# Layer 1's attention: TensorE's instructions in a written order, scores two pairs ahead, and a modulation block moved behind the first scores

## The chip, the cores and the metric

The kernel runs on one NeuronCore of a Trainium2 chip. The metric is the device time of one execution in microseconds (us), lower is better. The matrix engine is TensorE (PE in the profile, PEld its weight loads), VectorE is DVE, ScalarE is ACT, GpSimd is POOL, and SyncE (SP) issues the large weight loads. A name with a q (SPq, PEq) is an engine's instruction queue.

## The reference

The program computes two blocks in fp32 over 256 tokens of width 1024. The first block has two layers; the second has a recurrent mixer, a sparse attention and a mixture of experts. The change touches only the attention of layer 1 of the first block: 16 query heads in four groups, 256 tokens in two blocks of 128 queries, each with a window of local keys, 256 context keys and one sink logit per head.

```python
s_loc = jnp.einsum('bkgnqd,bkncd->bkgnqc', qb, kb).astype(f32) * scale
s_loc = jnp.where(valid, s_loc, -jnp.inf)
s_ctx = jnp.einsum('bkgnqd,bkld->bkgnql', qb, k_c).astype(f32) * scale
m = jnp.maximum(jnp.maximum(jnp.max(s_loc, -1, keepdims=True), jnp.max(s_ctx, -1, keepdims=True)), s_sink)
e_loc = jnp.exp(s_loc - m)
e_ctx = jnp.exp(s_ctx - m)
denom = jnp.sum(e_loc, -1, keepdims=True) + jnp.sum(e_ctx, -1, keepdims=True) + jnp.exp(s_sink - m)
o = (jnp.einsum('bkgnqc,bkncd->bkgnqd', e_loc, vb) + jnp.einsum('bkgnql,bkld->bkgnqd', e_ctx, v_c)) / denom
y = merge_heads(window_attention(q, k, v, k_c, v_c, od_sink[j])) @ od_w_out[j]
```

Beside it stands the modulation of the layers: `silu(c) @ w_mod + b_mod`, a vector times large weight matrices, which the kernel computes in blocks of 512 columns spread over the program.

## The kernel before

A tile framework turns the program into five instruction streams: it tracks the data dependencies, adds the semaphores and, for each engine, picks the order by priority (program order, unless a priority is raised) as operands and buffers come free in its plan. So the order on an engine is not the order of the lines; parts of one step can be cut up and mixed with others. Only at the end of the program (the experts) TensorE and SyncE are put in written order with `manual_schedule`.

The attention of layer 1 works on 16 pairs `(cb, tq, m)`: two query heads at a time, 128 queries, 512 keys. For a pair i there are:

- `a_scores` (L1143, L1146): for each of the two heads three matmuls of 64 rows by 512 columns (head 0 on rows 0 to 63 of the array, head 1 on rows 64 to 127; three because operands are split in a high and a low part) into a tile `s` of two PSUM banks, then two bf16 matmuls that add the window mask. There are two `s` tiles.
- `a_max` (L1152 to L1154), on VectorE: the row maximum of both heads, its minimum with the negated sink, and the difference that the sink's exponential needs.
- `a_exp` (L1161 to L1166): on ScalarE two exponentials of 512 columns that also sum up, and one of two columns for the sink; on VectorE the sum (L1163), the reciprocal (L1164) and two scalings of 512 columns (L1166).
- `a_turn` (L1172): eight transposes on TensorE into `pt`, of which there is one tile of two banks.
- `a_evac`: two copies of `pt` to SBUF on ScalarE.
- `a_av` (L1186): eight value matmuls (16 instructions), at a raised priority; after the fourth pair of a group ScalarE and VectorE write the result `o` as a high and a low part (L1190, L1191).

ScalarE's instructions appear under L244 and splits under L251, since helpers record them. The loop is written with scores one pair ahead. At i = 11 GpSimd fetches five row tiles and combines them (`x_of`, L886 and L887). At i = 16, behind the last pair, `fill(1)` puts in one modulation block (`mods_ev`, L398): 32 matmuls (64 instructions) over two 1 MB tiles that SyncE loaded (`wload`, L259, a ring of five `wr` buffers), a bias row, and an addition on VectorE (L400).

After the attention come the output projection (`mm_t`, L344 to L346), two more modulation blocks and the feed-forward part of layer 1.

Of the kernel before, what the change touches and what calls it, by code (L numbers as in the profile page):

```python
# [13 lines left out]
AF = mybir.ActivationFunctionType  # L14
# [102 lines left out]
def emit(tc, I, out, taps=None, stop=None):  # L117
# [64 lines left out]
    def t4(dt=F32, shape=(128, 1024)):  # L182
        return ap_.tile(list(shape), dt, name=nm("t4_"), tag="b4", bufs=NB["b4"])
# [59 lines left out]
    def act(o, i, fn, **k):  # L243
        return ac.activation(o, i, fn, **k)  # L244
# [622 lines left out]
    def brow1024(src_ap, eng=None):  # L867
        t_ = t4()
        (eng or po).dma_start(t_, bass.AP(tensor=src_ap.tensor, offset=src_ap.offset, ap=[[0, 128], [1, 1024]]))
        return t_  # L870
# [13 lines left out]
    def x_of(z, rows):  # L884

        po.tensor_tensor(z, z, rows[0], op=OP.mult)  # L886
        po.tensor_tensor(z, z, rows[1], op=OP.add)  # L887

    def tok_rows(d, t):
        return d[t * 128:(t + 1) * 128, :]  # L890
# [3 lines left out]
        ve.tensor_mul(tmp, ps, gate[:, cs])  # L894
        ve.scalar_tensor_tensor(z[:, cs], z[:, cs], ALPHA, tmp, op0=OP.mult, op1=OP.add)

    NF = (0, 2.2, 1, 2, 2, (16,))

    fills = [(1, 0), (1, 2), (1, 1), (1, 3), (1, 4), (1, 5), (1, 6), (1, 8), (1, 7), (1, 9), (2, 0), (2, 2), (2, 1), (2, 3),
             (2, 4), (1, 10), (1, 11), (2, 5), (2, 6), (2, 8), (2, 7), (2, 9), (2, 10), (2, 11)]  # L900
# [234 lines left out]
    def a_scores(i):  # L1135
        cb, tq, m = pairs[i]
        s_ = T_[i]["s"] = pst("s", (128, 2, 512))
        qs = slice(m * 256 + tq * 128, m * 256 + tq * 128 + 128)
        ks = slice(cb * 512, cb * 512 + 512)
        for hd in range(2):  # L1140
            pr = slice(64 * hd, 64 * hd + 64)
            for j, (qp, kp) in enumerate(((0, kTh), (0, kTl), (1, kTh))):
                pe.matmul(s_[:, hd], qT[cb][qp][pr, qs], kp[pr, ks], start=j == 0, stop=False, skip_group_check=True)  # L1143
        wc = slice(128, 256) if tq == 0 else slice(0, 128)
        for hd in range(2):
            pe.matmul(s_[:, hd, wc], identb, wmb[:, tq], start=False, stop=True, skip_group_check=True)  # L1146

    def a_max(i):
        cb, tq, m = pairs[i]
        nmx = T_[i]["nmx"] = sm((128, 4))  # L1150
        nsk = nsink[:, cb * 8 + 2 * m:cb * 8 + 2 * m + 2]
        ve.tensor_reduce(nmx[:, 0:2], T_[i]["s"], axis=AX.X, op=OP.max, negate=True)  # L1152
        ve.tensor_tensor(nmx[:, 0:2], nmx[:, 0:2], nsk, op=OP.min)
        ve.tensor_sub(nmx[:, 2:4], nmx[:, 0:2], nsk)  # L1154

    def a_exp(i):
        s_, nmx = T_[i]["s"], T_[i]["nmx"]
        e, den = t4(), sm((128, 4))
        T_[i]["e"] = e
        for hd in range(2):  # L1160
            act(e[:, HF[hd]], s_[:, hd], AF.Exp, bias=nmx[:, hd:hd + 1], accum_out=den[:, hd:hd + 1])  # L1161
        act(den[:, 2:4], nmx[:, 2:4], AF.Exp)
        ve.tensor_add(den[:, 0:2], den[:, 0:2], den[:, 2:4])  # L1163
        ve.reciprocal(den[:, 0:2], den[:, 0:2])  # L1164
        for hd in range(2):
            ve.tensor_scalar(e[:, HF[hd]], e[:, HF[hd]], den[:, hd:hd + 1], None, op0=OP.mult)  # L1166

    def a_turn(i):
        pt = T_[i]["pt"] = pst("t", (128, 4, 2, 128))
        for hd in range(2):  # L1170
            for c in range(4):
                pe.transpose(pt[:, c, hd], T_[i]["e"][:, c128(4 * hd + c)], ident)  # L1172

    def a_evac(i):
        pT = T_[i]["pT"] = t4(F32, (128, 4, 2, 128))
        act(pT[:, 0:2], T_[i]["pt"][:, 0:2], AF.Copy)
        act(pT[:, 2:4], T_[i]["pt"][:, 2:4], AF.Copy)

    def a_av(i):
        cb, tq, m = pairs[i]  # L1180
        o = T_[i]["o"] = pst("o", (128, 4, 128)) if m == 0 else T_[i - 1]["o"]
        with tc.high_priority(60):
            for c in range(4):
                for hd in range(2):
                    v0 = c * 256 + (2 * cb + hd) * 64
                    pe.matmul(o[64 * hd:64 * hd + 64, m, :], vT[:, v0:v0 + 64], T_[i]["pT"][:, c, hd], start=c == 0,  # L1186
                              stop=c == 3, skip_group_check=True, tile_position=(0, 64 * hd))
        if m == 3:
            hi, lo = aT.span(cb * 4, 4, tq * 128, tq * 128 + 128)
            act(hi, o, AF.Copy)  # L1190
            ve.tensor_sub(lo, o, hi.bitcast(F32))  # L1191

    N_ = len(pairs)
    a_scores(0)
    a_max(0)
    for i in range(N_ + 1):
        if i + 1 < N_:
            a_scores(i + 1)
        if i < N_:
            a_exp(i)  # L1200
        if i >= 1:
            a_evac(i - 1)
        if i + 1 < N_:
            a_max(i + 1)
        if i >= 1:
            a_av(i - 1)
        if i < N_:
            a_turn(i)
        if i == 11:
            g1 = brow1024(mods_dram[1][0, 2048:3072])  # L1210
            lnr = [brow1024(I["ln_g"][0, 1]), brow1024(I["ln_b"][0, 1])]
            z = [t4() for _ in range(2)]
            for t in range(2):
                po.dma_start(z[t], tok_rows(xres1, t))
                x_of(z[t], lnr)
        if i in NF[5]:
            fill(1, lambda shape: pst("o", shape))
    psum_tags(g=4, x=4)

    tap("aT0", aT.hi[0].bitcast(F32))  # L1220
# [1114 lines left out]
```

## Time and profile before

| | us |
|---|---|
| median of 3 executions | 1558.17 (1555.2 to 1563.67) |
| the profiled execution | 1555.63 |
| its span, first to last instruction | 1553.9 |
| TensorE busy | 1440.3 (93%) |
| VectorE busy | 971.8 (63%) |
| ScalarE busy | 549.2 (35%) |
| GpSimd busy | 263.7 (17%) |

The profile is of one execution; 1.7 us of its time lie outside of the span. [...] A busy TensorE in the records is not one at its peak: ends of matmuls are modelled and overlap, so the distance between starts is what to read. Averages over the span say little on one stage; the attention is read from its own windows.

### The profile page before, as it was taken

To read this page: it belongs to the slowest core of one execution; us is meant where nothing else is said; L and a number is where in the kernel's file an instruction comes from. 1 tells how busy PE (TensorE), PEld (TensorE's weight loads), DVE (VectorE), ACT (ScalarE), POOL (GpSimd) and SP (SyncE) were. 2 spreads that over 40 slices of the span, in tenths; PEclk is the share of its full clock that TensorE was granted. 3 is DMA by queue.
4 is the path that set the end of the run, shared out by engine and by line. 5 is a ranking of instruction groups with operands and counts; after the bars stand their busy time and mean duration, and the time that the engine had idled before them with its cause. 6 is when DMAs were issued, how large, how long until landed. Compare 5 with 4: busy or idle time off the path is not lost. (4 is left out here: it accounts for less than half of the span.)

```text
span 1553.9 us, 22193 instructions
## 1 busy us (share of the span) xinstructions
PE 1440.3 (93%) x8651; PEld 1081.8 (70%) x8651; DVE 971.8 (63%) x1662; ACT 549.2 (35%) x921; POOL 263.7 (17%) x263
## 2 busy tenths in 40 slices
PE   5999899999999999989889899997898897999896
PEld 3688687798887778869657898986787675532332
DVE  2443797789999887685665766566688446112212
ACT  2443233353223223234454455545554333301001
POOL 0032204100132210321130410003425320000000
PEclk9998999999999999999889999998999798999999
DMA  8740564446779876526323965564334746699996
GB/s 290 261 167 1 190 244 143 162 151 216 236 258 326 279 239 224 207 72 191 84 69 107 331 214 190 190 213 154 116 110 138 255 152 240 251 410 410 411 410 259
DMA packets 189395, 332.96 MB, mean 214 GB/s; under 512 B 12666, under 2 KB 67554, under 8 KB 189283
## 3 DMA queue, kind: packets, MB, share of 16 engines
q1 hardware_dynamic: 175152, 298.77, 55.4%
q0 software_dynamic: 8640, 27.85, 5.1%
q10 hardware_dynamic: 5490, 4.85, 1.1%
q8 instruction: 70, 1.15, 0.3%
q14 instruction: 43, 0.34, 0.1%
HBM read 320.91 MB, written 10.53 MB: 213 GB/s over the span
## 5 line engine op out<-in xcount | busy, mean ns | idle before, releaser
L251 DVE TENSOR_TENSOR wl<-wr,wh 128x1024 fp32r<-128x1024 f32 (+1 forms) x206 | 254.1, 1247 | 65.8 <-ACT wh L244 63.9
L244 ACT ACTIVATE wh<-wr 128x1024 fp32r<-128x1024 f32 (+1 forms) x226 | 228.8, 1027 | 176.0 <-PE g L346 91.3
L344 PE MATMUL g<-wh,h 128*128 128x512 f32 (+1 forms) x624 | 247.5, 399 | 13.0 <-DVE t L1396 7.1
L319 PE MATMUL g<-h,wh 128*128 128x256 f32 (+1 forms) x768 | 251.7, 329 | 3.5 <-DVE t L1031 2.4
L321 PE MATMUL g<-h,wl 128*128 128x256 f32 (+1 forms) x768 | 250.2, 327 | 3.8 <-DVE wl L251 3.8
L320 PE MATMUL g<-h,wh 128*128 128x256 f32 (+1 forms) x768 | 251.2, 328 | 0.2 <-DVE h L251 0.2
L345 PE MATMUL g<-wl,h 128*128 128x512 f32 (+1 forms) x624 | 244.9, 393 | 2.6 <-DVE wl L251 2.6
L346 PE MATMUL g<-wh,h 128*128 128x512 f32 (+1 forms) x624 | 244.2, 393 | 2.0 <-DVE h L1701 2.0
L427 DVE SCALAR_TENSOR_TENSOR t<-wr,cT,t 128x512 f32<-128x512 f32 x231 | 172.8, 785 | 14.2 <-DMA wr<-w_mod_in 7.0
L319 PEld LDWEIGHTS g<-h,wh 128*128 128x128 f32 x768 | 147.3, 192 | 20.0 <-DVE t L1031 3.7
L321 PEld LDWEIGHTS g<-h,wl 128*128 128x128 f32 x768 | 147.2, 192 | 17.2 <-DVE wl L251 5.1
L320 PEld LDWEIGHTS g<-h,wh 128*128 128x128 f32 x768 | 147.6, 192 | 12.5 <-DVE h L251 0.6
L344 PEld LDWEIGHTS g<-wh,h 128*128 128x128 f32 x624 | 119.2, 192 | 42.9 <-issue 10.1
L345 PEld LDWEIGHTS g<-wl,h 128*128 128x128 f32 x624 | 119.2, 191 | 26.9 <-DVE wl L251 3.8
L346 PEld LDWEIGHTS g<-wh,h 128*128 128x128 f32 x624 | 118.8, 190 | 27.1 <-DVE h L1701 3.0
L244 ACT ACTIVATE t<-t 128x512 f32<-128x512 f32 (+7 forms) x83 | 47.3, 592 | 129.3 <-DVE t L2163 73.6
L244 ACT ACTIVATE h<-e 128x512 fp32r<-128x512 f32 (+1 forms) x64 | 33.5, 524 | 146.1 <-DVE e L962 146.1
L251 POOL TENSOR_TENSOR wl<-wr,wh 128x1024 fp32r<-128x1024 f32 x20 | 50.4, 2519 | 192.2 <-ACT wh L244 180.4
L244 ACT ACTIVATE t<-x 128x128 f32<-128x128 f32 (+3 forms) x78 | 30.7, 464 | 145.0 <-PE x L2139 109.7
L244 ACT ACTIVATE e<-g 128x512 f32<-128x512 f32 (+1 forms) x72 | 35.6, 494 | 95.2 <-PE g L321 85.6
L241 POOL TENSOR_TENSOR sm<-sm,mhalf 128x1 f32<-128x1 f32 (+2 forms) x33 | 33.1, 1004 | 160.9 <-DVE sm L238 122.7
L2132 PE MATMUL g<-wr,t 128*32 128x512 f32 (+1 forms) x248 | 49.9, 596 | 6.3 <-DMA wr<-w_in 6.1
(429 smaller groups left out, 2180.1 us busy)
## 6 DMA issues: line engine op xcount, KB each, us to landing
wr<-mlp_w_in SPq DMA_DIRECT2D x64, 1024.0 KB
wr<-w_mod_in SPq DMA_DIRECT2D x40, 1024.0 KB
wr<-w_in SPq DMA_DIRECT2D x32, 1024.0 KB
t<-w_in SPq DMA_DIRECT2D x52, 512.0 KB
wr<-w_ada_in SPq DMA_DIRECT2D x24, 1024.0 KB
wr<-w_in_in SPq DMA_DIRECT2D x16, 1024.0 KB
wx<-w_in SPq DMA_DIRECT2D x14, 1024.0 KB
wh<-w_in SPq DMA_DIRECT2D x24, 512.0 KB
```

The costliest lines, as they stand in the source:

```text
L241: return po.tensor_tensor(o, o, mhalf[:, :o.shape[1]], op=OP.pow)
L244: return ac.activation(o, i, fn, **k)
L251: (leng or ve).tensor_sub(lo, src, hi.bitcast(F32))
L319: pe.matmul(ps, ah, bh, start=start, stop=False)
L320: pe.matmul(ps, ah, bl, start=False, stop=False)
L321: pe.matmul(ps, al, bh, start=False, stop=stop)
L344: pe.matmul(ps, ah[:, tsl], w[0][:, cs], start=start, stop=False)
L345: pe.matmul(ps, ah[:, tsl], w[1][:, cs], start=False, stop=False)
L346: pe.matmul(ps, al[:, tsl], w[0][:, cs], start=False, stop=stop)
L427: ve.scalar_tensor_tensor(s_, S["v"][:, k % 4], c_, s_, op0=OP.mult, op1=OP.add)
L2132: pe.matmul(ps[c:c + n, :], xg[p][k][:, c:c + n], w[a][k], start=k == 0, stop=k == 7, skip_group_check=True, tile_position=(0, c))
```

## The change

It rewrites the order of the loop and puts TensorE in written order in it. Scores and maxima of two pairs come first, then the modulation block that stood behind the last pair, then the exponentials of pair 0. In the loop, pair i is normalised (a function of its own now, ahead of the maximum of pair i + 2), scores are written two pairs ahead, transposes of pair i follow, then the maximum of i + 2, the exponentials of i + 1, the evacuation of i and the value matmuls of i - 1. In `a_exp` the sink's exponential goes ahead of the two large ones. The raised priority of the value matmuls goes away. Tiles, buffers and arithmetic stay.

```diff
-    NF = (0, 2.2, 1, 2, 2, (16,))
+    NF = (0, 2.2, 1, 2, 2)
...
-        T_[i]["e"] = e
+        T_[i]["e"], T_[i]["den"] = e, den
+        act(den[:, 2:4], nmx[:, 2:4], AF.Exp)
         for hd in range(2):
             act(e[:, HF[hd]], s_[:, hd], AF.Exp, bias=nmx[:, hd:hd + 1], accum_out=den[:, hd:hd + 1])
-        act(den[:, 2:4], nmx[:, 2:4], AF.Exp)
+
+    def a_norm(i):
+        e, den = T_[i]["e"], T_[i]["den"]
         ve.tensor_add(den[:, 0:2], den[:, 0:2], den[:, 2:4])
...
-        with tc.high_priority(60):
-            for c in range(4):
-                for hd in range(2):
+        for c in range(4):
+            for hd in range(2):
...
-    a_scores(0)
-    a_max(0)
-    for i in range(N_ + 1):
-        if i + 1 < N_:
-            a_scores(i + 1)
-        if i < N_:
-            a_exp(i)
-        if i >= 1:
-            a_evac(i - 1)
-        if i + 1 < N_:
-            a_max(i + 1)
-        if i >= 1:
-            a_av(i - 1)
-        if i < N_:
-            a_turn(i)
-        if i == 11:
...
-        if i in NF[5]:
-            fill(1, lambda shape: pst("o", shape))
+    with tc.manual_schedule(engines={mybir.EngineType.PE}):
+        for i in range(2):
+            a_scores(i)
+            a_max(i)
+        fill(1, lambda shape: pst("o", shape))
+        a_exp(0)
+        for i in range(N_ + 1):
+            if i < N_:
+                a_norm(i)
+            if i + 2 < N_:
+                a_scores(i + 2)
+            if i < N_:
+                a_turn(i)
+            if i + 2 < N_:
+                a_max(i + 2)
+            if i + 1 < N_:
+                a_exp(i + 1)
+            if i < N_:
+                a_evac(i)
+            if i >= 1:
+                a_av(i - 1)
+            if i == 11:
...
```

## Rows read from the trace of the kernel before

**Rows 1.** Window over the attention: us, each engine's busy time (instructions), clock, DMA share, GB/s
```profile
754.00:836.40 82.40, 73.20 (x577) 49.20 (x577) 52.05 (x121) 44.06 (x117) 12.12 (x9) 0.86 0.20 63
```

**Rows 2.** Timeline of TensorE at both ends: start, us, what, idle before it
```profile
754.24 0.98 PE L1143 MATMUL s<-h,h 64*128 64x512 f32 x6 [1.05 <-DVE t L1088]
...
759.26 1.65 PE L1143 MATMUL s<-h,h 64*128 64x512 f32 x5 [1.96 <-ACT t L244]
...
826.60 0.29 PE L1146 MATMUL s<-wmb,identb 128*128 128x128 bf16 x2
...
836.37 0.50 PE L344 MATMUL g<-wh,h 128*128 128x512 f32 x1 [1.42 <-DVE h L1191]
```

**Rows 3.** Timeline of two pairs in the middle, and the value matmuls of a later one
```profile
774.93 1.09 PE L1186 MATMUL o<-t,t 128*64 128x128 f32 x16
775.86 0.16 DVE L1154 TENSOR_TENSOR sm<-sm,nsink 128x2 f32<-128x2 f32 x1
775.96 1.09 PE L1172 MATMUL t<-c_ident,t 128*128 128x128 f32 x8
776.98 0.96 PE L1143 MATMUL s<-h,h 64*128 64x512 f32 x4
777.87 0.28 PE L1146 MATMUL s<-wmb,identb 128*128 128x128 bf16 x2
778.09 0.95 PE L1143 MATMUL s<-h,h 64*128 64x512 f32 x3
778.98 1.09 PE L1186 MATMUL o<-t,t 128*64 128x128 f32 x16
...
780.00 0.73 PE L1143 MATMUL s<-h,h 64*128 64x512 f32 x2
...
795.07 1.09 PE L1186 MATMUL o<-t,t 128*64 128x128 f32 x16
```

**Rows 4.** Windows inside the attention: PE, PEld, DVE, ACT, POOL, clock, DMA share, GB/s
```profile
754.00:770.00 16.00, 13.80 (x64) 8.79 (x64) 8.81 (x21) 7.10 (x20) 0.00 (x0) 0.57 0.21 67
760.00:765.00 5.00, 5.00 (x20) 2.74 (x18) 2.93 (x7) 1.81 (x5) 0.00 (x0) 0.50 0.00 1
775.00:795.00 20.00, 20.00 (x161) 13.36 (x160) 13.14 (x37) 13.39 (x36) 2.76 (x5) 1.00 0.36 116
795.00:805.00 10.00, 5.82 (x51) 3.80 (x50) 9.97 (x10) 4.88 (x13) 9.37 (x4) 0.91 0.08 32
800.00:815.00 15.00, 11.42 (x65) 7.89 (x64) 8.81 (x16) 6.54 (x17) 4.60 (x2) 0.66 0.01 2
```

**Rows 5.** Timeline around GpSimd's row operations
```profile
802.33 2.34 POOL L887 TENSOR_TENSOR t<-t,t 128x1024 f32<-128x1024 f32 x1
802.39 2.30 DVE L1154 TENSOR_TENSOR sm<-sm,nsink 128x2 f32<-128x2 f32 x1
...
805.24 1.94 PE L1172 MATMUL t<-c_ident,t 128*128 128x128 f32 x8 [2.93 <-DVE t L1166]
```

**Rows 6.** Groups of instructions in the attention: count, busy us, mean ns, idle before
```profile
L244 ACT ACTIVATE t<-s,sm 128x512 f32<-128x512 f32 x32 | 21.7, 684 | 15.8 <-DVE sm L1153 10.8 <-DVE sm L1164 3.4 <-DVE sm L1154 1.6
L1152 DVE TENSOR_REDUCE sm<-s 128x2 f32<-128x1024 f32 x16 | 19.5, 1222 | 18.1 <-PE s L1146 18.1
L244 ACT ACTIVATE t<-t 128x512 f32<-128x512 f32 x32 | 17.3, 597 | 11.2 <-PE t L1172 9.4 <-issue 1.8
L1166 DVE TENSOR_SCALAR t<-t,sm 128x512 f32<-128x512 f32 x32 | 14.1, 483 | 0.3
```

**Rows 7.** Timeline: loads of the attention's block, and a like block's matmuls later
```profile
702.05 22.63 SPq L259 DMA_DIRECT2D wr<-w_ada_in  x2
...
858.36 1.95 PE L398 MATMUL g<-wr,cT 128*32 128x128 f32 x64
```

**Rows 8.** Waits of SyncE's queue in the attention: us in total, times, longest
```profile
SPq L259 <- PE o L398: 77.4, 2, 73.3
```

**Rows 9.** Timeline of ScalarE behind the attention
```profile
886.06 2.01 ACT L244 ACTIVATE wh<-wr 128x1024 fp32r<-128x1024 f32 x2 [3.75 <-DMA wr<-mlp_w_in]
```

More of the change, by code (lines that the diff above doesn't have):

```diff
@@ L1181, in a_av @@
         o = T_[i]["o"] = pst("o", (128, 4, 128)) if m == 0 else T_[i - 1]["o"]
-        with tc.high_priority(60):
-            for c in range(4):
-                for hd in range(2):
-                    v0 = c * 256 + (2 * cb + hd) * 64
-                    pe.matmul(o[64 * hd:64 * hd + 64, m, :], vT[:, v0:v0 + 64], T_[i]["pT"][:, c, hd], start=c == 0,
-                              stop=c == 3, skip_group_check=True, tile_position=(0, 64 * hd))
+        for c in range(4):
+            for hd in range(2):
+                v0 = c * 256 + (2 * cb + hd) * 64
+                pe.matmul(o[64 * hd:64 * hd + 64, m, :], vT[:, v0:v0 + 64], T_[i]["pT"][:, c, hd], start=c == 0,
+                          stop=c == 3, skip_group_check=True, tile_position=(0, 64 * hd))
         if m == 3:
@@ L1193, in emit @@
     N_ = len(pairs)
-    a_scores(0)
-    a_max(0)
-    for i in range(N_ + 1):
-        if i + 1 < N_:
-            a_scores(i + 1)
-        if i < N_:
-            a_exp(i)
-        if i >= 1:
-            a_evac(i - 1)
-        if i + 1 < N_:
-            a_max(i + 1)
-        if i >= 1:
-            a_av(i - 1)
-        if i < N_:
-            a_turn(i)
-        if i == 11:
[L1210 to L1215, printed above, removed]
-        if i in NF[5]:
-            fill(1, lambda shape: pst("o", shape))
+    with tc.manual_schedule(engines={mybir.EngineType.PE}):
[20 more added lines that the diff above has]
+            if i == 11:
+                g1 = brow1024(mods_dram[1][0, 2048:3072])
+                lnr = [brow1024(I["ln_g"][0, 1]), brow1024(I["ln_b"][0, 1])]
+                z = [t4() for _ in range(2)]
+                for t in range(2):
+                    po.dma_start(z[t], tok_rows(xres1, t))
+                    x_of(z[t], lnr)
     psum_tags(g=4, x=4)
```

## The prediction

> **What bounds the kernel now.** I read the slices of the page first, then windows around the changed lines, then the timeline of TensorE in them, then the waits. The attention of layer 1 runs from the first score matmul at 754.24 us to the first matmul of the output projection at 836.37 us [rows 1, 2]: 82.1 of 1553.9 us, with TensorE busy 73.2 of 82.4 us at a mean clock of 0.86 [rows 1]. Everything that the change can win directly lies in those two numbers. Away from its ends and from one stall, TensorE sets the pace there: the value matmuls of successive pairs start at 774.93 and, five pairs later, at 795.07 [rows 3], 4.03 us a pair, busy throughout. [...] From 795 to 805 it is busy only 5.82 of ten us [rows 4], because GpSimd's row operations of 2.34 us hold up VectorE: a subtraction of two columns takes 2.30 us at 802.39, and the transposes start at 805.24 after 2.93 us of waiting [rows 5]. A second half-clock stretch follows: a mean of 0.66 in 800 to 815 [rows 4], (1 - 0.66) x 15 x 2 = 10.2 us, and each half-clock microsecond of busy TensorE costs half a microsecond.
>
> **The change, part by part.**
>
> *Steady work per pair.* Transposes take 1.02 us (775.96 to 776.98), the value matmuls 1.03 (774.93 to 775.96), the two window masks 0.22 (777.87 to 778.09) [rows 3], so the six scores have 4.03 - 2.27 = 1.76 us today, in pieces that the planner cut. Fixed order runs them as one piece: three on the lower 64 rows of the array, then three on the upper. Six scores took 0.98 us at the start, four 0.96, three 0.95, two 0.73 [rows 2, 3]. So a piece costs what its longer half costs, and a further score on the same half adds about 0.23 us. Six in one line would take 0.95 + 3 x 0.23 - 0.06 = 1.58 us to the mask (0.06 is what 0.95 overlaps the next piece by: 778.09 to 778.98 is 0.89). If the third and the fourth, on different halves, go side by side it is 1.35; if the second half starts afresh, 2 x 0.89 = 1.78; interleaved it would be 0.92. I take 1.47, between the two middle readings. A pair then takes 1.47 + 0.22 + 2.05 = 3.74 us; bounds 3.2 and 4.05.
>
> [...]
>
> *Does anything wait in the fixed order?* A wait now holds up all of TensorE's later work. The transposes of pair i come two pairs after its scores: 2 x 3.74 = 7.5 us. Their chain is one maximum 1.22, two exponentials of 0.68, two scalings of 0.48 and five small steps (the sink's minimum and subtraction, the small exponential that now comes first, the sum, the reciprocal) at 0.2 with their gaps, by the 0.16 of one [rows 3, 6]: 4.5 us, and 7.4 with another maximum, its small steps and an evacuation (two of 0.60) in front in the queues. It fits by 0.1 us at worst. I cost it at nothing; without that cover the planner's one-pair lead returns, and with it 4.03 a pair. Moving the small exponential ahead of the two large ones puts the subtraction in front of them; ScalarE has that room, busy 13.39 of 20 us in 775 to 795 [rows 4]. The priority of the value matmuls that goes away had only TensorE's order to set.
>
> *The modulation block.* Its 64 matmuls take 1.95 us at full clock [rows 7], about 3.9 at half, and move from the gaps of the last pairs to behind the second scores, where the 1.96 us wait [rows 2] covers half of it. Its two 1 MB loads are long there, issued from 702.05 us on [rows 7], and the next load waits 73.3 us for its matmuls to free their buffers [rows 8]. Its bias row, its addition on VectorE and its bank move along. SyncE's queue wins: the two loads that wait for these buffers go out some 70 us earlier, where the DMA share is 0.00 (760 to 765) [rows 4].
>
> *Sum.* To the end of the last pair's masks TensorE has 16 score pieces with masks (27.0), 13 sets of transposes (13.3), 12 of value matmuls (12.3) and the block (1.9): 54.5 us at full clock. From the last masks on today's chain of maximum, exponentials, scaling, transposes, evacuation, value matmuls and split takes 9.77 us from the start of the masks [rows 2], 9.6 from their end; I take 9.7, as the small exponential goes ahead. That is 64.2 of 82.1 us. Half clock at the start is not caused in the changed lines, so I keep its 13.8 us, now filled with work: + 6.9 (bounds 0 and, below, much more). GpSimd's row operations stay where they are: today they cost 10 - 5.82 = 4.2 us; with scores two pairs ahead I take half, 2.0 (bounds 0 and 4.2), and no second half-clock stretch. 64.2 + 6.9 + 2.0 = 73.1, a gain of 9.0 us.
>
> *Behind the attention.* At 886.06 ScalarE had waited 3.75 us for a weight load [rows 9]. Two megabytes fewer in that DMA queue can win there between 0 and about that much; I take 1, as TensorE has split weights in hand. What follows depends on results and on freed buffers and moves with it. Total gain 10.0 us. Against the profiled execution's own 1555.63 us that gives 1545.6; that execution lies 2.5 us under the median of the three, so the median to expect is 1548.
>
> **The rivals.**
> 1. *The forecast*, 1548, own range 1543 to 1553. Chance 0.44.
> 2. *The start comes out better.* The block closes the gap at 757 us and the clock returns earlier (half as long: 3.5), the stall vanishes (2.0), the loads win 3 more: 1540. For it: full clock came back in both stretches while TensorE ran without a gap [rows 4]. Chance 0.16.
> 3. *The stall stays, or the pace doesn't fall.* Four row operations of 2.34 us hold each a step of VectorE's chain; three of seven steps of a pair can be held, and a margin of 0.1 us doesn't cover that. Then 2.2 us more of stall and again 10.2 us at half (5.1): 1555. Or the change doesn't do what it says: the scores cost 1.78 and the pace stays at 4.03, + 5.0: 1553. Chance 0.26. [...]
> 4. *Slower: the clock stays low.* Today both half-clock stretches lasted on for some 10 us after TensorE had begun to run without a gap, at 759.26 and 805.24 [rows 2, 4, 5]. The mixture of work that TensorE then runs is another one in the new order, with its longest piece on half of the array's rows, so the clock may rise later. The 10 us are used up when the first stretch lasts 20 us longer, 34 instead of 13.8; at 50 us it costs 18.1 and the time is 1566. Against it: at full clock the same mixture kept the clock at 1.00 in 775 to 795 [rows 4]. Chance 0.14.
>
> **How the numbers follow.** The likeliest case gives 1548. About 0.5% (7.8 us) is what a measurement of this kernel can tell from no change, so faster means under 1550.4. Faster: three quarters of case 1, nearly all of 2, a little of 3: 0.53. Slower: most of case 4: 0.13. Same: 0.34. The range takes in cases 1 and 3 and most of 2: 1539 to 1560.
>
> **What would show it.** Value matmuls 3.6 to 3.9 us apart at full clock, with one piece of six scores between; the modulation block's matmuls around 757 to 762 us with no wait behind them; the next loads on SyncE right after; the projection starting about 9 us earlier than 836.4; under 2.5 us of waiting beside GpSimd's row operations. The forecast is wrong if value matmuls stay 4.0 us apart, if the clock is at 0.50 past 775 us, or if TensorE waits in each pair for VectorE or ScalarE.

## The result and the profile after

The changed kernel takes 1538.21 us (median of 4, 1532.1 to 1544.36), the kernel before, measured beside it, 1556.68 (median of 4, 1550.43 to 1563.67): a ratio of 0.988 with a 95% interval of 0.984 to 0.992. It is faster by some 18 us where 10 were forecast, and 1538.2 lies under the low end of the range, 1539.

The profiled execution took 1539.3 us, its span is 1537.5. Line numbers behind the loop move by a few: masks are L1146 as before, transposes L1175, scalings L1169, value matmuls L1188, the split L1193.

Windows of the changed kernel, in the columns of rows 1 and 4 (us, then PE, PEld, DVE, ACT and POOL with their instructions, clock, DMA share, GB/s); the last row is the whole attention:

```profile
751.87:765.00 13.13, 12.54 (x143) 8.92 (x144) 11.64 (x29) 8.52 (x25) 0.00 (x0) 0.87 0.67 242
765.00:787.50 22.50, 22.50 (x244) 16.98 (x242) 20.54 (x54) 19.49 (x53) 2.76 (x5) 1.00 0.30 113
787.50:798.40 10.90, 7.12 (x44) 4.58 (x41) 10.69 (x12) 4.34 (x13) 9.62 (x4) 0.69 0.03 11
798.40:814.20 15.80, 13.25 (x153) 10.55 (x153) 10.55 (x28) 10.89 (x27) 0.00 (x0) 1.00 0.01 3
751.87:814.20 62.33, 55.41 (x577) 41.03 (x577) 53.43 (x120) 43.24 (x117) 12.38 (x9) 0.92 0.26 94
```

The attention lasts 62.3 us from its first score to the output projection, against 82.1 [rows 1, 2]: 19.8 us are won, and all of the result lies there. The granted clock is 1.00 (full) or 0.50 (half) in every stretch of the trace, so its mean gives the time at half: (1 - 0.87) x 13.13 x 2 = 3.4 us at the start, (1 - 0.69) x 10.90 x 2 = 6.8 us in the third window, 10.2 in all where rows 4 gave 13.8 and 10.2. The second window is the steady part. All three engines are nearly full in it: TensorE 22.50 of 22.50 us, VectorE 20.54, ScalarE 19.49.

TensorE and VectorE in one steady pair (start, us, engine, line, operation, out <- in); it answers rows 3:

```profile
774.38 1.09 PE L1188 MATMUL o<-t,t 128*64 128x128 f32 x16
775.40 0.97 PE L1143 MATMUL s<-h,h 64*128 64x512 f32 x6
775.81 0.88 DVE L1169 TENSOR_SCALAR t<-t,sm 128x512 f32<-128x512 f32 x2
776.31 0.29 PE L1146 MATMUL s<-wmb,identb 128*128 128x128 bf16 x2
776.44 1.06 PE L1175 MATMUL t<-c_ident,t 128*128 128x128 f32 x8
776.63 1.22 DVE L1152 TENSOR_REDUCE sm<-s 128x2 f32<-128x1024 f32 x1
777.44 0.77 PE L1188 MATMUL o<-t,t 128*64 128x128 f32 x10
```

Value matmuls of successive pairs start 3.06 us apart here and, from 762.28 to 786.52, 3.03 on average, against 4.03. The six scores take 0.91 us (775.40 to 776.31), hardly more than three of one head do alone (0.89 in rows 3). Taken one by one, their records in another pair start at 766.326 and 766.336, 766.664 and 766.674, 766.895 and 766.905: two by two, though three of the first head are written ahead of three of the second. The records don't name the head; but three of one head alone start 0.34 and 0.24 us apart (777.823, 778.164 and 778.404 in e5, below), so two that start 10 ns apart are read as one of each. The masks cost 0.13 us, as the transposes begin beside them; transposes and value matmuls cost 1.00 and, with the next pair's scores behind them, 1.02.

TensorE at the start (rows 2 and 4 show it before); [ ] is idle time and what ended it:

```profile
751.87 0.97 PE L1143 MATMUL s<-h,h 64*128 64x512 f32 x6 [1.05 <-DVE t L1088]
...
752.98 1.66 PE L1143 MATMUL s<-h,h 64*128 64x512 f32 x6
...
754.89 2.67 PE L398 MATMUL o<-wr,cT 128*32 128x128 f32 x64
757.50 0.98 PE L1143 MATMUL s<-h,h 64*128 64x512 f32 x6
...
761.29 1.06 PE L1175 MATMUL t<-c_ident,t 128*128 128x128 f32 x8 [0.59 <-DVE t L1169]
```

The block stands in the gap, 2.60 us long and at half clock until 756.43, and no wait follows it. The second six take 1.59 us at half clock, the third 0.91.

The same kernel around GpSimd's row operations; it answers rows 5:

```profile
787.73 2.35 POOL L886 TENSOR_TENSOR t<-t,t 128x1024 f32<-128x1024 f32 x1 [3.33 <-DMA t<-xres]
...
787.95 4.91 DVE L1169 TENSOR_SCALAR t<-t,sm 128x512 f32<-128x512 f32 x2
...
790.16 2.40 POOL L887 TENSOR_TENSOR t<-t,t 128x1024 f32<-128x1024 f32 x1
790.51 1.06 PE L1175 MATMUL t<-c_ident,t 128*128 128x128 f32 x4 [1.78 <-DVE t L1169]
...
792.91 1.12 PE L1175 MATMUL t<-c_ident,t 128*128 128x128 f32 x4 [1.34 <-DVE t L1169]
...
795.14 2.37 POOL L887 TENSOR_TENSOR t<-t,t 128x1024 f32<-128x1024 f32 x1
795.19 2.33 DVE L1166 TENSOR_TENSOR sm<-sm 128x2 f32<-128x2 f32 x1
```

Two scalings that take 0.88 us elsewhere take 4.91 (2.42 and 2.57, beside GpSimd operations of 2.35 and 2.40), and the transposes behind them come in two halves with 1.78 and 1.34 us of waiting. Of the 10.90 us of the third window, 4.05 are work at full clock (two times six scores and masks, one set of transposes, one of value matmuls: 1.03 + 1.03 + 0.97 + 1.02): the stall costs 6.85 us, half clock included. By the distances between starts some 4.2 of it are waiting (1.94, 1.45 and 0.82 us ahead of the three pieces of transposes) and 2.6 the half clock.

At the end, and on SyncE at the start, with two of its loads in the kernel before in the last line:

```profile
814.16 0.50 PE L344 MATMUL g<-wh,h 128*128 128x512 f32 x1 [1.42 <-DVE h L1193]
...
752.97 5.04 SPq L259 DMA_DIRECT2D wr<-w_ada_in  x3
...
829.12 4.94 SPq L259 DMA_DIRECT2D wr<-w_ada_in  x2
```

From the last masks (804.46) to the projection it takes 9.70 us. Of SyncE's next three loads the first goes out at 752.97, as one did at 755.35 before; the two that wait for the block's buffers go out at 756.76 and 757.64, before the change at 829.12 and 833.69. Behind the attention nothing is won that can be told. From the projection's start to the end of the span it takes 717.5 us before (1553.9 - 836.37) and 723.3 after (1537.5 - 814.16), and 714 to 728 in the profiles of e1 to e12, with no relation to what they change (e9, whose stage is the same as the changed kernel's, has the 714). So single executions of one kernel differ by some 10 us in parts that nobody touched, and the comparison of experiments below goes by the stage first, then by medians.

### The profile page after: what moved, and what is told of

It reads as the page before. It is cut to its first block, busy times and chain, and to the rows that moved or that the text cites. A ratio compares the mean times of both kernels' runs of the same rounds, so it can differ in the third digit from the quotient of the medians.

```text
span 1537.5 us, 22176 instructions
## 1 busy us (share of the span) xinstructions
PE 1425.8 (93%) x8651; PEld 1076.4 (70%) x8651; DVE 973.6 (63%) x1662; ACT 548.0 (36%) x921; POOL 265.4 (17%) x263
## 4 chain that ended last, share of the span: by engine, by line
PE 33%; DMA 8%; DVE 6%; issue 3%; POOL 2%; ACT 2%; SPq 0%; DVEq 0%; POOLq 0%; ACTq 0%
PE g L2138 5%; PE g L321 2%; PE g L320 2%; PE g L319 2%; PE x L2164 2%; DMA wh<-w_in 2%; PE g L344 2%; PE g L346 2%; PE g L345 2%; DMA wr<-w_in 2%; PE x L345 2%; DMA wx<-w_in 2%; PE x L346 2%; PE x L344 2%; DMA wr<-mlp_w_in 2%
## 5 line engine op out<-in xcount | busy, mean ns | idle before, releaser
L251 DVE TENSOR_TENSOR wl<-wr,wh 128x1024 fp32r<-128x1024 f32 (+1 forms) x206 | 255.6, 1254 | 65.9 <-ACT wh L244 63.8
L244 ACT ACTIVATE t<-t 128x512 f32<-128x512 f32 (+7 forms) x83 | 47.3, 591 | 133.2 <-DVE t L2169 73.1
```

The costliest lines, as they stand in the source:

```text
L251: (leng or ve).tensor_sub(lo, src, hi.bitcast(F32))
```

## The experiments

Thirteen kernels ran, each beside the kernel before. The attention's time is read from each profile as above, from the first score to the projection; the time at half clock adds up its stretches at clock 0.50. Each profile is of one execution. The profile of e13 is used for the order of its instructions alone.

| kernel | median us | ratio to before, 95% | attention us | of it at half clock |
|---|---|---|---|---|
| before | 1556.7 | 1 | 82.1 | 23.9 |
| changed | 1538.2 | 0.984 to 0.992 | 62.3 | 10.2 |
| e1 all scores cut in two pieces | 1597.2 | 1.021 to 1.029 | 118.3 | 102.4 |
| e2 planner's order | 1542.2 | 0.988 to 0.994 | 65.2 | 13.7 |
| e3 block at the end | 1544.9 | 0.989 to 0.995 | 63.8 | 6.8 |
| e4 no row operations | 1532.1 | 0.982 to 0.990 | 55.4 | 3.3 |
| e5 cut from the ninth pair on | 1563.8 | 1.002 to 1.007 | 86.4 | 44.4 |
| e6 one pair ahead | 1566.9 | 1.004 to 1.010 | 85.5 | 23.9 |
| e7 row operations in quarters | 1533.5 | 0.981 to 0.988 | 57.8 | 0 |
| e8 row operations at the end | 1537.9 | 0.987 to 0.994 | 56.8 | 3.4 |
| e9 scores written in turns | 1539.1 | 0.986 to 0.993 | 62.5 | 10.2 |
| e10 cut in pairs 2 to 5 | 1554.1 | 0.995 to 1.001 | 80.2 | 37.3 |
| e11 before, lead and priority alone | 1548.5 | 0.991 to 0.997 | 68.7 | 6.8 |
| e12 e7 and e8 together | 1534.0 | 0.982 to 0.990 | 55.8 | 3.4 |
| e13 before, lead alone | 1553.0 | 0.995 to 1.000 | – | – |

### e1: the second head's scores behind the transposes

```diff
...
             if i + 2 < N_:
-                a_scores(i + 2)
+                a_scores(i + 2, (0,))     # first head
             if i < N_:
                 a_turn(i)
             if i + 2 < N_:
+                a_scores(i + 2, (1,))     # second head, masks
                 a_max(i + 2)
```

> The changed kernel with one edit: from pair 2 on, the three scores of the first head are written ahead of the transposes and those of the second head with the masks behind them. Theory A (the six scores win because the threes of both halves of the array stand together and run side by side, 0.91 us for six): each three now costs 0.89 by itself, value matmuls stand 3.9 us apart instead of 3.03, the attention takes some 12 us longer than 62.3 and the time is about 1550. Rival B (the gain is in the longer lead of the scores and fewer waits, not in the score matmuls): the pace stays near 3.0 and the time near 1538.

It took 1597.2 us, 59 more than the changed kernel; theory A had the price of the cut, but neither theory foresaw the clock. Windows of it (line numbers of e1, e5 and e10 are higher by two): the start, the long middle, the tail:

```profile
759.33:771.40 12.07, 9.52 (x108) 6.25 (x109) 8.51 (x21) 6.02 (x19) 0.00 (x0) 1.00 0.73 262
771.40:873.80 102.40, 96.23 (x434) 65.59 (x435) 44.82 (x98) 36.81 (x96) 12.17 (x9) 0.50 0.08 26
873.80:877.60 3.80, 2.42 (x37) 1.99 (x35) 0.69 (x1) 1.68 (x3) 0.00 (x0) 1.00 0.02 4
```

After a wait of 1.69 us the clock falls to half at 771.4 and stays there for 102.4 us, with TensorE busy in 96.23 of them. A pair takes 7.28 us at half: 1.58 for each three scores, 1.90 for transposes, 1.90 for value matmuls, 0.32 for masks. Full clock comes back only behind the last scores. So two things must be told apart: what the cut costs by itself, and what it does to the clock.

### e5: the same cut, from the ninth pair on

Against e1:

```diff
-                a_scores(i + 2, (0,))
+                a_scores(i + 2, (0,) if i + 2 >= 8 else (0, 1))
...
-                a_scores(i + 2, (1,))
+                if i + 2 >= 8:
+                    a_scores(i + 2, (1,))
```

> The changed kernel, but from the ninth pair on the second head's three scores and the masks stand behind the transposes; the first eight pairs keep six scores together, and no gap of TensorE lies ahead of the first cut pair. Price of the cut alone, at full clock: 3 + 3 scores 0.9 us each against 0.91 for six, so + 0.9 us in eight pairs, + 7.2 on the changed kernel's 1538: 1545. Theory A (the cut costs only its own time; the clock falls only behind a gap): clock at 1.00 in the ninth and tenth pair, pace about 3.95 us there, and half clock only from GpSimd's row operations on; if it then doesn't return before the loop ends, some four pairs at 7.3 instead of 3.9, + 14: between 1545 and 1559. Theory B (cut pieces lower the clock by themselves): half clock soon after the ninth pair's scores, eight pairs at 7.3 us, + 34: about 1572.

It took 1563.8 us, above theory A's range. Windows before and after GpSimd's row operations begin to stall it:

```profile
778.00:791.50 13.50, 12.08 (x96) 8.16 (x96) 7.28 (x18) 7.84 (x21) 2.77 (x5) 1.00 0.54 160
795.80:836.80 41.00, 38.59 (x181) 26.90 (x182) 17.53 (x42) 14.71 (x38) 6.23 (x3) 0.50 0.00 1
```

Theory A in kind: entered at full clock, cut pairs keep 1.00. But they take 4.76 us each (value matmuls at 780.96, 785.73, 790.49), not 3.95: 3.03 + 0.89 for the second three + 0.10 for masks that have nothing to run beside + 0.75 of waiting, since the maximum starts later and the scalings come later (0.68 us waiting for them in each pair). Then the row operations make TensorE wait (2.65 us ahead of the transposes at 795.12), the clock falls at 795.8, and it doesn't return until 836.8, in the last transposes; no score runs any more. That stretch of 41.0 us is the same behaviour as in e1.

### e10: the cut in pairs 2 to 5 alone

Against e1:

```diff
-                a_scores(i + 2, (0,))
+                a_scores(i + 2, (0,) if i + 2 < 6 else (0, 1))
...
-                a_scores(i + 2, (1,))
+                if i + 2 < 6:
+                    a_scores(i + 2, (1,))
```

> The changed kernel, but in pairs 2 to 5 the second head's scores and the masks stand behind the transposes; all other pairs keep six scores together. TensorE enters this stretch at half clock, or falls to it at the wait of the second transposes. Theory A (the clock comes back only where the six run whole): half clock through the four cut pairs, 7.3 us each, and full soon after the seventh pair's scores, some 5 us later: 4 x 4.25 + 2 = + 19, 1557. Theory B (the clock comes back some time after TensorE runs without a gap, whatever it runs): half clock for 3.4 to 10 us as in the kernels before and after, cut pairs at 4.77 us as in the late cut: 4 x 1.74 + 2 = + 9, 1547.

The median is 1554.1 us; the executions spread from 1545.5 to 1562.2. In the profiled one, TensorE in the last cut pair and the first whole one:

```profile
779.23 1.97 PE L1177 MATMUL t<-c_ident,t 128*128 128x128 f32 x8
781.13 1.65 PE L1145 MATMUL s<-h,h 64*128 64x512 f32 x3
782.71 0.40 PE L1148 MATMUL s<-wmb,identb 128*128 128x128 bf16 x2
783.03 1.97 PE L1190 MATMUL o<-t,t 128*64 128x128 f32 x16
784.94 1.65 PE L1145 MATMUL s<-h,h 64*128 64x512 f32 x6
786.52 0.28 PE L1148 MATMUL s<-wmb,identb 128*128 128x128 bf16 x2
786.64 1.04 PE L1177 MATMUL t<-c_ident,t 128*128 128x128 f32 x8
```

and its windows on both sides:

```profile
766.00:786.50 20.50, 20.50 (x95) 13.46 (x93) 8.00 (x21) 7.88 (x21) 0.00 (x0) 0.50 0.01 2
786.50:800.00 13.50, 13.50 (x144) 10.33 (x144) 12.12 (x30) 10.73 (x30) 2.23 (x4) 1.00 0.30 80
```

Half clock lasts 20.5 us without one gap of TensorE and ends with the first six scores that stand together: they take 1.59 us, the masks behind them run at full clock, and so does what follows, up to the row operations. Theory A for this execution. At its start, ahead of the cut pairs, it had run otherwise:

```profile
752.60 1.65 PE L1145 MATMUL s<-h,h 64*128 64x512 f32 x6 [1.05 <-DVE t L1088]
...
754.51 1.66 PE L1145 MATMUL s<-h,h 64*128 64x512 f32 x6
...
756.43 3.28 PE L398 MATMUL o<-wr,cT 128*32 128x128 f32 x64
```

There two whole sixes run at half clock, and full clock comes back only in the block behind them, at 759.21, after 6.8 us: a whole six doesn't end half clock each time. The lowest executions, near 1546, are at what theory B asks for; they may have entered the cut pairs at full clock as e1 did at first, but no trace shows that.

### e3: the block at the end again

```diff
-        fill(1, lambda shape: pst("o", shape))
         a_exp(0)
...
                 a_turn(i)
+            if i == N_ - 2:
+                fill(1, lambda shape: pst("o", shape))
```

> The changed kernel with the modulation block between the transposes of pair 14 and the value matmuls of pair 13 instead of behind the first scores. Theory C (the block fills the gap for the first exponentials and so the clock returns after 3.4 us instead of 13.7): a gap of about 1 to 2 us behind the second scores, a half-clock stretch of 10 us or more at the start again, 5 us of it lost; the block hides 1 us of waiting at the end: about 1543. Rival D (the clock returns early because scores in pieces of six load TensorE otherwise than before, the block only fills time): 3.4 us of half clock as in the changed kernel, 1538 to 1540.

It took 1544.9 us. TensorE at its start:

```profile
758.74 1.43 PE L1143 MATMUL s<-h,h 64*128 64x512 f32 x6 [1.05 <-DVE t L1088]
...
760.43 1.66 PE L1143 MATMUL s<-h,h 64*128 64x512 f32 x6
...
763.84 0.98 PE L1143 MATMUL s<-h,h 64*128 64x512 f32 x6 [1.43 <-ACT t L244]
```

The wait is back (1.43 us), but the third six run at 0.91, so full clock is back by 763.84 with no block in the gap: half clock is 3.4 us at the start here too. So rival D holds for the clock, though its 1538 to 1540 us weren't reached. The block doesn't bring the clock back; it saves its own place, 1.9 us in the tail, and costs 2.6 at the start in a gap of 1.4. The stage lasts 63.8 us against 62.3, with a smaller stall this time.

### e11 and e13: two edits of the kernel before

```diff
     a_max(0)
+    a_scores(1)
     for i in range(N_ + 1):
-        if i + 1 < N_:
-            a_scores(i + 1)
         if i < N_:
             a_exp(i)
+        if i + 2 < N_:
+            a_scores(i + 2)
...
-        with tc.high_priority(60):       # e11 alone; e13 keeps it
```

> The kernel before with two edits alone: scores are written two pairs ahead (behind the exponentials of the pair that frees their tile), and the value matmuls lose their raised priority. TensorE's order stays the planner's, the block stays behind the last pair, normalising and the sink's exponential stay. In its order the six scores of every pair stand together. Theory A (together they are the gain, the rest is worth little): pace 3.0 to 3.1 us, half clock at the start 3.4 us as with the block behind, a stall beside GpSimd's row operations as in the changed kernel: 1541 to 1546. Theory B (without the written order and the earlier normalising the transposes come late): 0.5 us or more of waiting in each pair, pace 3.5 or more, 1550.

It took 1548.5 us, stage 68.7. The six scores of each pair stand together in the planner's order, and the value matmuls start 3.17 us apart (764.38, 767.55, 770.73, 773.90). The 0.14 us to the changed kernel are masks that stand ahead of value matmuls instead of transposes (0.22 against 0.12) and transposes at 1.02. At the start TensorE waits 2.78 us behind the second masks, the next six run at half, 1.59 us, and full clock is back in the transposes behind them: 3.4 us at half, where the kernel before, after 1.96 us of waiting, ran five of its six scores in one piece [rows 2] and had 13.8 us. Theory A with a larger stall (1.64 and 3.66 us behind two pairs' masks). So these two edits alone bring 13.4 of the 19.8 us of the stage (82.1 to 68.7).

> The kernel before with scores two pairs ahead alone; the value matmuls keep their raised priority and cut each pair's scores in the planner's order in four (three of the first head, one of the second) and two, with the value matmuls between; maximum and masks follow the two. Theory A (the cut costs its own time, and a piece in which both halves of the array still run side by side for a while lets the clock return as it did in the kernel before): 0.96 + 0.73 us for four and two instead of 0.91, pace 3.9 to 4.0 us a pair at full clock, half clock at the start for 10 to 14 us, attention 80 us: 1553 to 1558. Theory B (any cut of the six holds the clock down as three and three did): half clock to the last pair, 7 us a pair, 1590 or more. Theory C (only the lead was missing, the cut is covered): 1545 to 1550 as without the raised priority.

It took 1553.0 us (0.995 to 1.000), theory A's lower edge. In the order of its instructions nearly every pair has four scores, sixteen value matmuls, two scores. So the lead alone is worth 3 to 4 us by the medians, though its interval reaches from almost nothing to 8, and together with the dropped priority, which lets the six stand together, 8 (the two medians against 1556.7). What the dropped priority is worth without the lead wasn't run.

### e2: the planner's order for the rewritten lines

```diff
-    with tc.manual_schedule(engines={mybir.EngineType.PE}):
+    with ExitStack():
```

> The changed kernel without the written order on TensorE: the lines stand as in the changed kernel, the planner picks the order. Theory A: the planner takes the scores apart again as before the change, pieces of about 0.9 us between transposes and value matmuls, 4.0 us a pair, 1550 to 1555. Rival (the rewriting of the lines, lead and priority, already gives the good order): pieces of six, 3.0 us a pair, 1538.

It took 1542.2 us, stage 65.2. The planner puts the six together by itself and reaches 3.03 us a pair. What it loses, 2.9 us of the stage, is a larger stall beside the row operations: the first wait there is 5.31 us instead of 1.78. That need not come of the planner's order, as the same wait took 3.53 us in e9 and 4.55 in e10, both in written order. The medians (1542.2 and 1538.2) can't be told apart, so no gain of the written order by itself is shown.

### e9: the six scores written in turns

```diff
-        for hd in range(2):
-            pr = slice(64 * hd, 64 * hd + 64)
-            for j, (qp, kp) in enumerate(((0, kTh), (0, kTl), (1, kTh))):
+        for j, (qp, kp) in enumerate(((0, kTh), (0, kTl), (1, kTh))):
+            for hd in range(2):
+                pr = slice(64 * hd, 64 * hd + 64)
```

> The changed kernel with the six scores of a pair written in turns, one for each head, instead of three of the first head and then three of the second. Theory A (what counts is that scores of both halves of the array stand next to one another; the array takes the other half's beside the running ones by itself): the same 0.91 us for six, pace 3.03, 1538. [...]

1539.1 us, stage 62.5. A piece of six and the masks behind it:

```profile
765.37 0.96 PE L1143 MATMUL s<-h,h 64*128 64x512 f32 x6
766.27 0.28 PE L1146 MATMUL s<-wmb,identb 128*128 128x128 bf16 x2
```

Six scores take 0.90 us, at the same pace: theory A. Two records that start together are now up to 4 ns apart instead of 10. How the six are written doesn't matter as long as they stand together.

### e6: one pair ahead

```diff
-        for i in range(2):
-            a_scores(i)
-            a_max(i)
+        a_scores(0)
+        a_max(0)
...
-            if i + 2 < N_:
-                a_scores(i + 2)
+            if i + 1 < N_:
+                a_scores(i + 1)
...
-                a_max(i + 2)
+                a_max(i + 1)
```

> The changed kernel with the scores written one pair ahead instead of two; TensorE still in written order, six scores together. Theory A (the lead of two is needed by a fixed order): between the end of a pair's scores and its transposes stand maximum 1.2, exponentials 1.5 to 2, sum, reciprocal and scalings 1.2, together about 4.5 us, and TensorE has only transposes, value matmuls and the next scores, 2.9 us, to run meanwhile; pace 4.7 to 5 us a pair instead of 3.03, with 1.6 to 2 us of waiting for the scalings in each, + 25: 1563, more if these gaps lower the clock. Theory B (only the six adjacent scores count, the lead is a spare): pace stays near 3.03, 1538.

It took 1566.9 us, slower than before. Waits of TensorE in its attention (engine, line, releaser: us, times, longest):

```profile
PE t L1175 <- ACT t L244: 13.1, 8, 4.3
PE t L1175 <- DVE t L1169: 10.4, 5, 4.0
```

Together 23.5 us in 13 waits, in 12 of 16 pairs, all ahead of the transposes. At full clock a pair takes 4.3 us (value matmuls at 772.11, 776.38, 780.65) with 1.2 us of waiting: theory A, a little under its pace, and the time at half clock adds the rest. A written order needs the lead of two; it can't run something else meanwhile.

### e4, e7, e8, e12: the row operations

e4 leaves the four operations out, e7 cuts each in four, e8 moves loads and operations behind the last pair, e12 does both.

```diff
                     po.dma_start(z[t], tok_rows(xres1, t))
-                    x_of(z[t], lnr)                          # e4: left out
+                    for c in range(4):                       # e7, e12
+                        cs = slice(256 * c, 256 * c + 256)
+                        x_of(z[t][:, cs], [r_[:, cs] for r_ in lnr])
...
-            if i == 11:
+            if i == N_:                                      # e8, e12
```

> The changed kernel without GpSimd's four row operations at i = 11: the residual's rows are left without their scale and offset, so its output isn't the reference's. It prices the stall that is left: 787.5 to 798.4 us holds 4.05 us of TensorE's work at full clock and takes 10.9. Theory: the stall and its half-clock stretch go away, 6.8 us, attention 55.5, time 1531. Rival: something else (VectorE at 2.7 of 3.03 us a pair) takes its place and at most 3 us are won.

> The changed kernel with each of GpSimd's four row operations cut in four of 256 columns, about 0.6 us each. Theory A (VectorE is held for one GpSimd instruction at a time, so shorter ones hold it shorter): the longest held VectorE step falls from 4.9 and 2.3 us to under 1.3, TensorE's stall of 6.8 us falls to 2 to 3 and the half-clock stretch behind it goes: 1533 to 1535. Theory B (the hold is a share of the time for as long as GpSimd works, whatever the size): the same 6.8 us, 1538, or more if sixteen instructions take longer than four.

> The changed kernel with GpSimd's five row loads and four row operations written behind the last pair instead of the twelfth. Theory A (the stall is a matter of where they fall): no stall inside the loop, pace 3.03 to the end, no half-clock stretch there; one or two steps of the tail (a scaling, the split ahead of the projection) are held by up to 2.3 us: 1533 to 1536. Theory B (the tail has no cover, and each of four holds falls on its chain or on the projection's first residual step): as slow as before the move or slower, 1538 to 1545.

> The changed kernel with GpSimd's row loads and row operations behind the last pair, and each row operation cut in four of 256 columns. Theory A: no stall in the loop, and the last scaling, held by 2.1 us when the operations are whole, is held by 0.6 at most: attention 55.5 us from the first score to the projection against 56.8 with whole ones and 57.8 with quarters behind the twelfth pair: 1531 to 1533. Theory B (the operations now lie beside the projection's splitting and residual steps on VectorE, which they hold for as long as they work): 2 us are lost again there, 1533 to 1538.

Without them (e4) the attention takes 55.4 us, 6.9 less, and runs at 3.03 to its end: that is the price of the stall, and it agrees with the 6.85 read above. Its window over the attention:

```profile
752.82:808.26 55.44, 52.25 (x577) 39.08 (x577) 46.49 (x120) 43.13 (x117) 2.77 (x5) 0.97 0.31 106
```

In quarters (e7):

```profile
795.66 1.43 POOL L886 TENSOR_TENSOR t<-t,t 128x256 f32<-128x256 f32 x2 [5.73 <-DMA t<-xres]
795.75 0.65 DVE L1154 TENSOR_TENSOR sm<-sm,nsink 128x2 f32<-128x2 f32 x1
796.71 1.52 DVE L1169 TENSOR_SCALAR t<-t,sm 128x512 f32<-128x512 f32 x2
...
797.51 0.63 PE L1175 MATMUL t<-c_ident,t 128*128 128x128 f32 x4 [0.20 <-DVE t L1169]
```

A held two-column step takes 0.65 us instead of 2.33, a pair of scalings 1.52 instead of 4.91, and the transposes wait for a scaling by at most 0.23 us inside the loop; the clock is 1.00 throughout. GpSimd is busy longer (12.1 us for the sixteen against 9.6 for the four), and that costs nothing that can be seen: the stage is 57.8. Theory A. At the end (e8) the loop runs free and one scaling of the tail is held, 2.98 us for the last two, so the stage is 56.8, theory A by the stage and not by the median; in quarters at the end (e12):

```profile
801.21 1.60 POOL L886 TENSOR_TENSOR t<-t,t 128x256 f32<-128x256 f32 x2 [3.95 <-DMA t<-xres]
801.24 1.85 DVE L1169 TENSOR_SCALAR t<-t,sm 128x512 f32<-128x512 f32 x2
...
807.12 0.50 PE L344 MATMUL g<-wh,h 128*128 128x512 f32 x1 [1.42 <-DVE h L1193]
```

55.8, 0.3 from the stage without any: theory A by the stage, while the median, 1534.0, lies 1 us above its range. The medians of e7 and e12, 1533.5 and 1534.0, lie 4 to 6 us under the changed kernel's 1538.2 and e9's 1539.1, which has the same stage; e8's 1537.9 doesn't, against a stage 5.5 us shorter. Intervals overlap, so the stage is what shows the gain, and the medians only go the same way for e7 and e12.

## Why the prediction missed, step by step

**The bound** was read rightly: TensorE set the pace, and the gain lies inside the two ends that rows 1 and 2 gave. By terms the forecast's 73.1 us became 62.3: work 11.0 less, tail the same, start 4.6 less, stall 4.9 more.

**The score piece is the step that failed.** It was taken as 1.47 us; it took 0.91, the reading that the prediction called interleaved and left as an outer bound. That alone is 16 x 0.56 = 9.0 us. With masks at 0.12 instead of 0.22 (1.6 us more) the pair takes 3.03 instead of 3.74, and work at full clock up to the last masks 43.5 us instead of 54.5 (52.6 from 751.87 to 804.46, less 6.85 for the stall and 2.25 at the start). The evidence stood in the rows: six scores in 0.98 [rows 2] is the very case, and its records start two by two, 10 ns apart for the first two, as after the change. A model for pieces (the longer half, 0.23 for a further score) was put over it, with the written order as the reason to think that at most the third and the fourth run side by side; that was the author's estimate, and no run shows it. e9 shows that the order within the six is worth nothing, e1 and e5 that three of the second head placed elsewhere cost 0.89 more. The first half of that model was right: a piece costs its longer half, and the longer half of six is three.

**No waits in the fixed order**: right in the steady part, where TensorE is busy 22.50 of 22.50 us. The margin was thin in another way than reckoned: VectorE has 2.0 us in 22.5 to spare at the new pace. e6 shows what stands behind "costs nothing": with half the lead TensorE waits in 12 pairs and the kernel is slower than before.

**The block**: the gap is closed, and the two loads that waited for its buffers leave at 756.76 and 757.64, 72 and 76 us earlier, as forecast. But rival 2's reason, that the closed gap returns the clock, falls with e3: it returns as early with the gap open. That its 1540 lies nearest to the result is luck: of its terms only the better start came, while the stall stayed and the loads won nothing that can be told.

**Half clock at the start**: kept at 13.8 us, which rows 4 give as (1 - 0.57) x 16 x 2, it was 3.4; the start cost 2.25 us over its work at full clock, not 6.9: 0.68 for the second six (1.59 - 0.91), 0.10 for their masks, 0.71 for the block (2.60 against 1.89 in e12, at full clock), and 0.76 until the second transposes get their scalings. Not all of the 2.25 is the clock's price: e7 ran the same start at full clock throughout, TensorE waited 0.82 us for the first exponentials instead, and its second transposes began 9.02 us after the first score against 9.42. The prediction said that it isn't caused in the changed lines. The runs speak for a fall that comes from ahead of them (in the kernel before behind waits of 1.08 and 1.05 us, at 752.50 and 754.24) and a length that depends on them, but of the kernel before there is one profile alone. The start of the changed kernel, which e2, e4, e5, e7, e8, e9 and e12 share, spent 0 (e7) to 3.4 us at half, and 6.8 in e10. After a similar wait e11 has 3.4 us with the six together, the kernel before 13.8 with cut ones; e10 ends its 20.5 us with the first whole six behind the cut pairs, though two at its start had not ended half clock; e1 has none behind its fall and never comes back while scores run. What the runs leave open is why: the clock also came back among transposes and value matmuls without scores, in the tails of e1 (873.8) and e5 (836.8), and cut pairs entered at full clock kept it (1.00 in e5 from 778.00 to 791.50, and the kernel before in 775 to 795 [rows 4]).

**The stall** was taken as 2.0 us without a second half-clock stretch; it cost 6.85 with one of 6.8 us. Rival 3's mechanism was right, with its reason that a margin of 0.1 us covers no hold of 2.3: the waiting is the 4.2 us of the kernel before again, of which two pairs' lead was to cover half. Its price for the half clock, 5.1 us, was too high; the 6.8 us at half cost 2.6. In the kernel before the held steps were small ones with two tensor inputs, which take 0.15 or 0.16 us elsewhere:

```profile
795.82 1.72 DVE L1153 TENSOR_TENSOR sm<-sm,nsink 128x2 f32<-128x2 f32 x1
...
798.06 1.91 DVE L1154 TENSOR_TENSOR sm<-sm,nsink 128x2 f32<-128x2 f32 x1
...
801.02 1.25 DVE L1163 TENSOR_TENSOR sm<-sm 128x2 f32<-128x2 f32 x1
```

With the 2.30 of rows 5 these are the three of seven steps that rival 3 counts. The changed kernel shows more: its scalings, with one tensor input, are held as well, 4.91 us for two that take 0.88 alone. A maximum beside GpSimd (792.77) isn't, at 1.21 us against 1.22 elsewhere; it reads its scores from the PSUM tile `s`, and why it is spared was not shown. In quarters the hold follows the length of GpSimd's instruction (0.65 us beside two of 0.72 each, against 2.33 beside one of 2.37).

**The tail**: 9.7 forecast, 9.70 measured. **Behind the attention**: 1 us forecast; ScalarE waits 4.05 us there for the same weight load (3.75 before [rows 9]), so the earlier loads didn't relieve it.

**Rival 4**, half clock through the loop, didn't happen, but its mechanism is real and larger than priced: e1 spends 102.4 us at half, where 50 were put for 1566. It lay in the other order of the same matmuls, the cut one, not in this one. The longest piece on half of the array's rows, named as its reason, turned out to be no such piece.

So two errors made the forecast 16 us too slow (the steady work 11.0, of it 9.0 the score piece; the start 4.6), and one, the stall, 4.9 us too fast: together the 10.8 by which the stage came out shorter. That the median missed by no more than 10 us owes something to this second error with the other sign.

## What to carry to other kernels

Where a row of the trace shows the very piece that a new order will run, its time goes ahead of any model built from its neighbours. Scores of two heads that use different halves of the array should stand together: apart they cost twice (0.89 for each three against 0.91 for six), and in e1 and e5 TensorE, once at half clock, stayed there for as long as they ran apart (102.4 and 41.0 us). When all three engines are filled to nine tenths, look for the one long instruction elsewhere that holds one of them, and try to cut it into short ones (here 62.3 to 57.8 us of the stage).

## What was not expected of the hardware

- Six matmuls of 64 rows, three for each half of the array, take the time of three (0.91 us, written in turns 0.90, against 0.89), also when three of one half stand ahead of three of the other.
- TensorE stayed at half clock for 102.4 us while it was busy in 96.2 of them (e1), 41.0 (e5, busy in 38.6), and 20.5 without one gap (e10). In e10 it came back to full clock at the end of the first six scores that stood together (1.59 us from 784.94); at the start of the same execution two such pieces didn't bring it back (6.8 us at half). Why it stays is open.
- GpSimd operations of 2.34 to 2.53 us held up not only VectorE steps with two tensor inputs (up to 2.33 us for two columns that take 0.16) but scalings with one (2.42 and 2.57, 0.88 for two alone), each for about one GpSimd instruction.
